# Where the triangular solve of the gated DeltaNet branch is started among the forgetting-attention tiles of a hybrid encoder step

## The chip, the cores and the metric

The kernel runs on 1 core of a Trainium2 chip. The metric is the time of one execution on the device in microseconds (us). Five engines run their own instruction queues: TensorE (PE, with its weight loads shown as PEld), VectorE (DVE), ScalarE (ACT), GpSimd (POOL) and SyncE (SP, which issues most DMAs). Each works its queue in the order in which the program was built; semaphores hold an instruction until what it needs is there.

## The reference, cut to what matters

One layer for two request groups (a prompt of 1024 rows and a sample of 64 rows behind a cache of 256). Four branches read one projection of the normed input; then come their gates, the merge, the output projection and a SwiGLU block.

```python
def fox_core(q_args, q_pos, k, v, ck, k_pos):            # forgetting attention ("fox")
    s = einsum('bqhd,bkhd->bhqk', q, k) * HEAD_DIM ** -0.5
    s = s + cq[..., :, None] - ck[..., None, :]
    p = softmax(where(k_pos <= q_pos, s, -inf))
    return einsum('bhqk,bkhd->bqhd', p, v)
...
a = p[:, :, 0] - lam * p[:, :, 1]                        # differential attention ("diff")
...
m = where(strict, einsum('nbhid,nbhjd->nbhij', kb, kc) * decay, 0.0)   # gated DeltaNet ("gdn")
sol = triangular_solve(m + eye(chunk), rhs, lower=True, unit_diagonal=True)
S, o = lax.scan(step, s0, (qc, kc, u0, kcum, gcum, qk))  # sequence over the 64-row chunks
...
merged = sum(gate[:, :, i] * (o @ wb[i]) for i, o in enumerate(branches))
```

## The kernel before, in words

Rows are worked in tiles of 128 (t = 0 to 7 of the prompt, t = 8 the sample). Attention runs branch by branch: sb (stick-breaking), then fox, then diff; within a branch by pair of heads (0, 1), within a pair over the tiles in the order 7, 6, 5, 4, 3, 2, 8, 1, 0. A tile t of the prompt has W = 128 (t + 1) keys, the sample 320. Below, "fox 0.4" is tile 4 of pair 0 of the fox branch.

A fox tile, for each of its two heads: PE writes scores into a PSUM bank `psc` (L456, L460; three such banks), DVE takes them out with one custom operation that adds the bias and keeps the running minimum ("score sum", L570), ACT takes the exponential, ACT and DVE write the two halves of the probability `st`, SP turns it with a transposing DMA into `pt`, and PE multiplies it with the values (`pv`, L468). A diff head takes four or two score banks, a maximum on DVE (L646, into `sm`), an exponential on ACT (L655, into `p`), some small DVE operations, `st`, the transposing DMA, and PE's `po` (L604, L606).

Between the attention instructions PE gets dense work that waits for nothing there: `spill_gates` computes the gates of all four branches in 96 pieces of 24 matmuls (`pgs`, L183 to L185), which ACT evicts as `ths` and POOL's queue writes to DRAM as `gtd`. A third stream is the list `side`: three generators, of which each call of `fill` advances the first by one step. `gdn_solve` loads the blocks `X` from DRAM (L871), does 30 steps of two DVE operations each (`tmpx` and `X`, L67) and stores the result (`xd`, `xtd`); `gdn_seq` then runs the sequence over 17 chunks on PE, DVE and ACT (`vn`, `vh`, `S32p`, `Sl`, `ztg`, `osg` are its DVE results); `open_merge` opens the pool of the merge and loads the sb branch's part of it. `fill` is called once in each fox tile and once in each diff head, before the multiplication with the values.

The merge comes last: 96 pieces of 6 matmuls (`ptb`), a tanh on ACT of the gate read back from DRAM (`thg`), and products and sums into `mg` on DVE and POOL. Its sb part (24 pieces) may start once `open_merge` has run; the fox, diff and gdn parts need the memory that attention gives back at its end.

The order on each engine isn't written out by hand: the code is traced, and a scheduler puts the traced instructions of each engine in an order by its own timeline, the earlier traced first among those it takes for ready. `issue_after(x)` forbids a block's instructions to stand ahead of `x` on the engine of `x`. So a step that is traced earlier shifts everything behind it.

Of the kernel before, what the change touches and what calls it, by code (L numbers as in the profile page):

```python
# [13 lines left out]
ALU = mybir.AluOpType  # L14
# [34 lines left out]
def rows(t):  # L49
    return P if t < 8 else SMP  # L50
# [3 lines left out]
def tile_hybrid_encoder(ctx, tc, i, o):  # L54

    nc = tc.nc
    act, vec, gps, pe, sync = nc.scalar, nc.vector, nc.gpsimd, nc.tensor, nc.sync


    def acopy(out, in_, scale=1.0):  # L60
        return act.activation(out, in_, AF.Copy, scale=scale)  # L61

    def stt(out, in0, s, in1, op0, op1):
        return vec.scalar_tensor_tensor(out=out, in0=in0, scalar=s, in1=in1, op0=op0, op1=op1)  # L64

    def tt(out, in0, in1, op, eng=None):
        return (eng or vec).tensor_tensor(out=out, in0=in0, in1=in1, op=op)  # L67

    def ts(out, in0, s1, s2, op0, op1=None, eng=None):
        if op1 is None:  # L70
            return (eng or vec).tensor_scalar(out=out, in0=in0, scalar1=s1, scalar2=None, op0=op0)  # L71
        return (eng or vec).tensor_scalar(out=out, in0=in0, scalar1=s1, scalar2=s2, op0=op0, op1=op1)

    def bc(ap, shape):
        return ap.to_broadcast(shape)
# [13 lines left out]
    def psc(name="psc"):  # L89
        return pp.tile([P, 512], F32, tag="s", name=name, bufs=3)  # L90
# [178 lines left out]
    for t in range(NT):  # L269
        n = rows(t)  # L270
# [45 lines left out]
    for t0, cols in (((0, 1, 2, 3), 0), ((4, 5, 6, 7), 512), ((9, 10, 8), 1024)):  # L316
        ps = psc("pct")
        c = 0
        for t in t0:
            n = SMP if t == 8 else P  # L320
# [107 lines left out]
    def qgeom(t):  # L428

        if t < 8:  # L430
            return P, 0, (t + 1) * P, [(j, P) for j in range(t + 1)]
        return SMP, SEQ, PAST + SMP, [(8, P), (9, P), (10, SMP)]

    def chunks(W):
        return [(c, min(512, W - c)) for c in range(0, W, 512)]

    def p_tiles(W, n):

        nb = (W + P - 1) // P
        st = at.tile([P, 2, 1024], F16, tag="st", name="st", bufs=3)  # L440
        sv = st.rearrange("p a b -> p (a b)")[:, :2 * nb * P].rearrange("p (a b) -> p a b", a=2)
        if W % P:
            vec.memset(sv[:n, :, W:], 0.0)
        pt = at.tile([P, 16, P], F16, tag="pt", name="pt", bufs=4)

        def transpose():
            sync.dma_start_transpose(out=pt[:, 0:2 * nb, 0:n], in_=sv[:n].rearrange("p a b -> p (a b)"))
            return lambda hl, j, ks: pt[:ks, hl * nb + j, 0:n]

        return sv, transpose  # L450

    def scores(ps, n, w, q0, q1, kk, col, mask, diag):

        two = q1 is not None
        last = mask is None and not two
        pe.matmul(ps[:n, :w], lhsT=q0, rhs=kk[:, col:col + w], start=True, stop=last)  # L456
        if mask is not None:
            pe.matmul(ps[:n, diag:diag + n], lhsT=identb[:n, :n], rhs=mask[:n, :n], start=False, stop=not two)
        if two:
            pe.matmul(ps[:n, :w], lhsT=q1, rhs=kk[:, col:col + w], start=False, stop=True)  # L460
# [14 lines left out]
    def load_kv(b, pair):  # L475
        nk = 4 if b == "diff" else 2
        kT = []
        for q in range(0, nk, 2):
            k2 = at.tile([P, 2, KW], F16, tag="k", name="kT", bufs=3)
            sync.dma_start_transpose(out=k2, in_=kd_[b][:, (pair * nk + q) * P:(pair * nk + q + 2) * P])  # L480
            kT += [k2[:, 0], k2[:, 1]]
        vt = at.tile([P, 11, 2, 2, 64], F16, tag="v", name="vt", bufs=2)
        v3_ = vt.rearrange("p t h l e -> p t (h l e)")
        cs = slice(pair * 256, (pair + 1) * 256)
        sync.dma_start(v3_[:, 0:10], vd[b][0:SEQ + PAST, cs].rearrange("(t p) c -> p t c", p=P))
        sync.dma_start(v3_[:SMP, 10], vd[b][SEQ + PAST:, cs])
        return kT, vt

    def load_q(b, pair, t, n):
        qt = at.tile([P, 4, P], F16, tag="qt", name="qt", bufs=3)  # L490
        sync.dma_start_transpose(out=qt[:, :, 0:n], in_=qd[b][t * P:t * P + n, pair * 512:(pair + 1) * 512])
        return qt


    dense, side = [], []
# [21 lines left out]
    at_mark = [None]  # L517
# [34 lines left out]
    def attend_fox():  # L552
        for pair in range(2):
            kT, vt = load_kv("fox", pair)
            ckb = cb.tile([P, 2, KW], F32, tag="ckb", name="ckb", bufs=1)
            for hp in range(2):
                gps.dma_start(ckb[:, hp], ckd[2 * pair + hp].partition_broadcast(P))
            for t in QORD:
                n, kc, W, vl = qgeom(t)
                qt = load_q("fox", pair, t, n)  # L560
                pts = []
                for hp in range(2):
                    s = at.tile([P, 1024], F32, tag="wk", name="s", bufs=6)
                    mn = at.tile([P, 4], F32, tag="sm", name="mn", bufs=6)
                    for c, (c0, w) in enumerate(chunks(W)):
                        ps = psc()
                        diag = W - n - c0 if c0 + w == W else None
                        scores(ps, n, w, qt[:, 2 * hp, :n], qt[:, 2 * hp + 1, :n], kT[hp], kc + c0,
                               mk_fox if diag is not None else None, diag)
                        vec.tensor_tensor_reduce(  # L570
                            out=s[:n, c0:c0 + w], in0=ps[:n, :w], in1=ckb[:n, hp, kc + c0:kc + c0 + w], scale=0.125,
                            scalar=(3e38 if c == 0 else mn[:n, c - 1:c]), op0=ALU.add, op1=ALU.min,
                            accum_out=mn[:n, c:c + 1])
                    act.activation(s[:n, :W], s[:n, :W], AF.Exp, scale=-1.0, bias=mn[:n, c:c + 1], accum_out=mn[:n, 2:3])
                    vec.reciprocal(mn[:n, 3:4], mn[:n, 2:3])
                    ts(mn[:n, 3:4], mn[:n, 3:4], PS, None, ALU.mult)
                    sv, tr = p_tiles(W, n)
                    acopy(sv[:n, 0, :W], s[:n, :W], mn[:n, 3:4])
                    at_mark[0] = stt(sv[:n, 1, :W], s[:n, :W], mn[:n, 3:4], sv[:n, 0, :W], ALU.mult, ALU.subtract)
                    pts.append(tr())  # L580
                fill(FILL_FOX * W)
                pv_pair("fox", pair, t, n, vt, vl, pts)
# [281 lines left out]
    def gdn_solve():  # L864


        NP = 17 * NH
        with tc.tile_pool(name="gp2", bufs=1, side="right", reuse_waits="tile") as g2p:
            X = g2p.tile([NP, 2, 32, 32], F32, name="X")
            tmp = g2p.tile([NP, 512], F32, name="tmpx")  # L870
            gps.dma_start(X.rearrange("p b j i -> p b (j i)"), nd[0:17, :, 0:2].rearrange("n h b j i -> (n h) b (j i)"))  # L871
            for _ in range(2):
                yield 0.0
            for j in range(1, 31):
                r = 31 - j
                behind = tc.issue_after(at_mark[0].ins) if j == 1 else ExitStack()
                behind.__enter__()
                tj = tmp[:, :2 * j * r].rearrange("p (b c i) -> p b c i", b=2, c=j)
                tt(tj, bc(X[:, :, 0:j, j:j + 1], [NP, 2, j, r]), bc(X[:, :, j:j + 1, j + 1:32], [NP, 2, j, r]), ALU.mult)
                tt(X[:, :, 0:j, j + 1:32], X[:, :, 0:j, j + 1:32], tj, ALU.add)  # L880
                behind.__exit__(None, None, None)
                if j % 4 == 0:
                    yield 0.0
            for q in range(2):
                vec.memset(X[:, q].rearrange("p j i -> p (j i)")[:, 0:1024:33], 1.0)
            gps.dma_start(xd, X.rearrange("p b j i -> p (b j i)"))
            for q in range(2):
                vec.tensor_copy(tmp.rearrange("p (i j) -> p i j", j=32),
                                X[:, 0, :, 16 * q:16 * q + 16].rearrange("p j i -> p i j"))
                gps.dma_start(xtd[:, 512 * q:512 * q + 512], tmp)  # L890
# [231 lines left out]
    def open_merge():  # L1122
        gd_.close()
        brps.append(br_.enter_context(tc.tile_pool(name="br", bufs=1, side="right", reuse_waits="tile")))
        load_branch("sb")
        yield 0.0

    side += [gdn_solve(), gdn_seq(gd_), open_merge()]
    attend_fox()
    attend_diff()  # L1130
    drain(side)
# [154 lines left out]
    with tc.tile_pool(name="ps2", bufs=1, space=PSUM) as pf:  # L1286
# [189 lines left out]
        for t in (8, 0, 1, 2, 3, 4, 5, 6, 7):  # L1476
            n = rows(t)
# [54 lines left out]
```

## Time and profile before

| what | value |
|---|---|
| median of 3 runs | 1818.23 us (1810.99 to 1825.81) |
| profiled execution | 1816.62 us, span of its instructions 1814.9 us |
| granted TensorE clock, mean | 0.988 |
| PE busy | 1723.7 us (95%) |
| DVE busy | 1246.7 us (69%) |
| ACT busy | 866.9 us (48%) |
| POOL busy | 307.0 us (17%) |

The busy times are unions over the whole span. The stages differ: attention with the gates fills about 330 to 920 us, the merge about 920 to 1040 us, and after it come the output projection and the SwiGLU block, which the change doesn't touch.

### The profile page before, as it was taken

How to read it: one execution, taken by the hardware profiler on the slowest of the kernel's cores; microseconds unless marked ns; L12 is line 12 of the kernel's file. 1: busy time of each engine (PE TensorE's matmuls, PEld its weight loads, DVE VectorE, ACT ScalarE, POOL GpSimd, SP SyncE). 2: the span in 40 equal slices, each digit the busy share in tenths (PEclk: the TensorE clock that was granted, in tenths of full speed). 3: DMA queues.
4: the chain of work that ended last, by engine and by line, in shares of the span. 5: the costliest groups of instructions: out<-in, count | busy, mean ns of one | idle time of the engine just before them, and what ended most of it. 6: DMA issues, size and time to landing. Idle time of an engine off the chain costs nothing.

```text
span 1814.9 us, 36826 instructions
## 1 busy us (share of the span) xinstructions
PE 1723.7 (95%) x14364; PEld 1224.8 (67%) x14364; DVE 1246.7 (69%) x2589; ACT 866.9 (48%) x1819; POOL 307.0 (17%) x478
## 2 busy tenths in 40 slices
PE   7999898888998899999988899999999999999998
PEld 5678787765565566666655588768668578577573
DVE  7659875966678777877868877667555556365465
ACT  6336556986765465665665634424223124132132
POOL 2114241011121222322236611000000000000003
PEclk9999999998999999999999999999999999999999
DMA  7267689979699986765589555312112112112113
GB/s 231 50 100 200 205 239 243 212 181 180 142 226 199 184 199 149 160 154 147 122 280 290 165 154 109 88 49 64 52 47 71 47 47 70 35 36 70 35 48 105
DMA packets 412766, 244.28 MB, mean 135 GB/s; under 512 B 266278, under 2 KB 390450, under 8 KB 412456
## 3 DMA queue, kind: packets, MB, share of 16 engines
q1 hardware_dynamic: 398944, 205.67, 46.6%
q0 software_dynamic: 13648, 36.27, 7.1%
q8 instruction: 112, 1.84, 0.5%
q14 instruction: 62, 0.51, 0.1%
HBM read 123.39 MB, written 60.53 MB: 101 GB/s over the span
## 4 chain that ended last, share of the span: by engine, by line
PE 55%; DMA 6%; DVE 5%; issue 2%; ACT 1%; POOL 1%; SPq 0%; DVEq 0%; POOLq 0%; ACTq 0%
PE po L1454 12%; PE pgs L183 4%; PE pgs L185 4%; PE pgs L184 4%; PE pb L1337 3%; PE pb L1339 3%; PE pb L1338 3%; DMA pt<-st 3%; PE pa L1339 2%; PE pc L1338 2%; PE pa L1338 2%; PE pa L1337 2%; PE pc L1339 2%; PE pc L1337 2%; DMA thg<-gtd_sb 1%
## 5 line engine op out<-in xcount | busy, mean ns | idle before, releaser
L184 PE MATMUL pgs<-u,wh 128*128 128x364 f16 (+1 forms) x768 | 245.5, 320 | 0.0
L183 PE MATMUL pgs<-u,wh 128*128 128x364 f16 (+1 forms) x768 | 245.4, 319 | 0.0
L185 PE MATMUL pgs<-u,wl 128*128 128x364 f16 (+1 forms) x768 | 245.3, 319 | 0.0
L1454 PE MATMUL po<-wh,hT 128*128 128x512 f16 (+1 forms) x792 | 238.1, 380 | 0.6 <-DVE x2a L64 0.6
L1454 PEld LDWEIGHTS <-hT 128*128 128x128 f16 (+1 forms) x1188 | 109.2, 99 | 120.1 <-issue 7.6
L64 DVE SCALAR_TENSOR_TENSOR x2a<-po,x2a 128x512 f32<-128x512 f32 x108 | 74.4, 689 | 141.5 <-PE po L1454 141.3
L61 ACT ACTIVATE wh<-w32f 128x1024 f16<-128x1024 f32 (+1 forms) x90 | 80.3, 926 | 160.7 <-PE po L1454 111.7
L1337 PE MATMUL pb<-X,wh 128*128 128x288 f16 (+1 forms) x528 | 147.4, 280 | 2.5 <-DMA X<-nsh 2.2
L64 DVE SCALAR_TENSOR_TENSOR wl<-w32f,wh 128x1024 f16<-128x1024 f32 (+1 forms) x90 | 94.6, 1064 | 79.7 <-ACT wh L61 79.6
L1338 PE MATMUL pb<-X,wh 128*128 128x288 f16 (+1 forms) x528 | 147.7, 280 | 0.0
L1339 PE MATMUL pb<-X,wl 128*128 128x256 f16 (+1 forms) x528 | 146.8, 280 | 0.0
L1337 PEld LDWEIGHTS <-wh 128*128 128x128 f16 x1232 | 120.8, 98 | 31.6 <-issue 2.3
L1454 PE MATMUL po<-wl,hT 128*128 128x512 f16 (+1 forms) x396 | 142.0, 379 | 0.0
L1338 PEld LDWEIGHTS <-wh 128*128 128x128 f16 x1232 | 120.8, 98 | 30.3 <-issue 2.4
L1339 PEld LDWEIGHTS <-wl 128*128 128x128 f16 x1232 | 120.8, 98 | 27.0 <-issue 0.4
L165 PE MATMUL pd<-wh,u 128*128 128x256 f16 (+1 forms) x448 | 125.1, 279 | 4.4 <-DVE qs L64 2.3
L166 PE MATMUL pd<-wl,u 128*128 128x256 f16 (+1 forms) x448 | 125.0, 279 | 0.0
L167 PE MATMUL pd<-wh,u 128*128 128x256 f16 (+1 forms) x448 | 124.9, 279 | 0.0
L185 PEld LDWEIGHTS <-wl 128*128 128x128 f16 x912 | 89.7, 98 | 50.7 <-issue 2.7
L183 PEld LDWEIGHTS <-wh 128*128 128x128 f16 x912 | 89.8, 98 | 50.1 <-issue 0.7
L184 PEld LDWEIGHTS <-wh 128*128 128x128 f16 x912 | 89.8, 98 | 49.0 <-issue 0.9
L71 POOL TENSOR_SCALAR fss<-fss 128x1 f32<-128x1 f32 (+1 forms) x9 | 2.0, 220 | 661.8 <-ACT fsq L1483 661.8
(393 smaller groups left out, 4625.3 us busy)
## 6 DMA issues: line engine op xcount, KB each, us to landing
w<-in_w_in_dram SPq DMA_DIRECT2D x56, 512.0 KB, 5.0
w32f<-in_w_ffn_gate_dram SPq DMA_DIRECT2D x20, 512.0 KB, 5.0
w32f<-in_w_ffn_up_dram SPq DMA_DIRECT2D x20, 512.0 KB, 3.9
w32f<-in_w_ffn_down_dram SPq DMA_DIRECT2D x20, 512.0 KB, 4.3
xt<-in_x_prompt_dram SPq DMA_DIRECT2D x8, 512.0 KB, 6.7
wb<-in_w_branch_dram SPq DMA_DIRECT2D x8, 512.0 KB, 4.8
w<-in_w_out_dram SPq DMA_DIRECT2D x8, 512.0 KB, 5.4
x2a<-in_x_prompt_dram SPq DMA_DIRECT2D x8, 512.0 KB, 7.9
```

Of the source, the lines that this page charges most:

```text
L61: return act.activation(out, in_, AF.Copy, scale=scale)
L64: return vec.scalar_tensor_tensor(out=out, in0=in0, scalar=s, in1=in1, op0=op0, op1=op1)
L165: pe.matmul(ps[:n, :N], lhsT=a, rhs=wh[:, k, :N], start=(k == 0), stop=False)
L166: pe.matmul(ps[:n, :N], lhsT=a, rhs=wl[:, k, :N], start=False, stop=False)
L167: pe.matmul(ps[:n, :N], lhsT=b, rhs=wh[:, k, :N], start=False, stop=(k == K - 1))
L183: pe.matmul(ps[:, :n], lhsT=a, rhs=xh[:, k, off:off + n], start=(k == 0), stop=False)
L184: pe.matmul(ps[:, :n], lhsT=a, rhs=xl[:, k, off:off + n], start=False, stop=False)
L185: mm = pe.matmul(ps[:, :n], lhsT=b, rhs=xh[:, k, off:off + n], start=False, stop=(k == K - 1))
L1337: pe.matmul(ps[:, :n], lhsT=wh[:, k], rhs=xh_, start=(start and k == 0), stop=False, skip_group_check=not start)
L1338: pe.matmul(ps[:, :n], lhsT=wh[:, k], rhs=xl_, start=False, stop=False, skip_group_check=not start)
L1339: mm = pe.matmul(ps[:, :n], lhsT=wl[:, k], rhs=xh_, start=False, stop=(k == 3), skip_group_check=not start)
L1454: pe.matmul(ps[h * n:h * n + n], lhsT=hts[k + h][:, a, tk:tk + n], rhs=w[:, k + h], start=(k == 0 and a == 0 and w is wh), stop=(k + nh >= ...
```

## The change: what it does

It has three parts. `gdn_solve` yields once instead of twice behind its load of `X`. Its first step, which is that load, is taken with `next(side[0])` before fox is traced, so it stands ahead of fox's own loads. And the mark behind which the first solve step must stand (`at_mark`) is the last score sum of the tile instead of the last half of its probabilities. Together the solve's DVE steps are traced from the first fox tile on (before: from the third), and `gdn_seq` and `open_merge` move up by two calls of `fill` as well.

```diff
@@ attend_fox @@
-                        vec.tensor_tensor_reduce(
+                        at_mark[0] = vec.tensor_tensor_reduce(
                             out=s[:n, c0:c0 + w], in0=ps[:n, :w], in1=ckb[:n, hp, kc + c0:kc + c0 + w], scale=0.125,
...
-                    at_mark[0] = stt(sv[:n, 1, :W], s[:n, :W], mn[:n, 3:4], sv[:n, 0, :W], ALU.mult, ALU.subtract)
+                    stt(sv[:n, 1, :W], s[:n, :W], mn[:n, 3:4], sv[:n, 0, :W], ALU.mult, ALU.subtract)
@@ gdn_solve @@
-            for _ in range(2):
-                yield 0.0
+            yield 0.0
@@ tile_hybrid_encoder @@
     side += [gdn_solve(), gdn_seq(gd_), open_merge()]
+    next(side[0])
     attend_fox()
```

No instruction is added or removed; the order changes. Lines behind the first edit in `gdn_solve` are one lower in the changed kernel (L1067 becomes L1066) as far as `attend_fox()`.

DVE, the first tile of fox (7 of pair 0), from its last score sum (L570, the second row of which only reads its minimum out) on. Before:

```order
L570 ISA s,mn<-psc,ckb,mn 128x512
L570 ISA mn 128x1
L575 RECIPROCAL mn<-mn 128x1
L64 SCALAR_TENSOR_TENSOR os<-pv,os 128x128
L71 TENSOR_SCALAR mn<-mn 128x1
L570 ISA s,mn<-psc,ckb 128x512
```

Now:

```order
L570 ISA s,mn<-psc,ckb,mn 128x512
L570 ISA mn 128x1
L67 TENSOR_TENSOR tmpx<-X 68x60
L575 RECIPROCAL mn<-mn 128x1
L64 SCALAR_TENSOR_TENSOR os<-pv,os 128x128
L67 TENSOR_TENSOR X<-X,tmpx 68x2x30
L71 TENSOR_SCALAR mn<-mn 128x1
L67 TENSOR_TENSOR tmpx<-X 68x116
```

The solve starts right behind the first tile's score sums. Before the last `st` of fox 0.4 stood 10 of its 60 operations, now 30; before the last `st` of fox 0.1 stood 22, now 50.

PE, from the last gate matmul (`pgs`) on, at the end of attention (LDWEIGHTS are weight loads). Before:

```order
L185 MATMUL pgs<-u_103,wl 128x360
L183 LDWEIGHTS wbh
L183 MATMUL ptb<-oT,wbh 128x364
L184 LDWEIGHTS wbh
L184 MATMUL ptb<-oT,wbh 128x364
```

Now:

```order
L606 MATMUL po<-vt,pt 128x64
L456 LDWEIGHTS qt
L456 MATMUL psc<-kT,qt 128x384
L458 LDWEIGHTS identb
L458 MATMUL psc<-mk_diff,identb 128x128
```

Before, the sb part of the merge follows the last gate and only the last three `po` groups of diff (of pair 1: second head of tile 1, both heads of tile 0) stand among it. Now the piece shown stands 36 rows behind the last gate: behind that gate come 8 `ptb`, the last `po` of diff 1.4, and then the 16 scores of diff 1.2, 1.8, 1.1 and 1.0 with all their `po` and those of diff 1.3 (62 `po` matmuls in all, 8 before). Ahead of the last `po` stand 11 `ptb` pieces now, 9 before, and 14 `ptb` matmuls have moved ahead of the last gate.

ACT, the eviction of the last gate piece (`ths`) and what is next to it; `sm_12700` holds the sums of the first head of diff 1.2, `sm_12763` of its second, `sm_12620` of diff 1.3's second. Before:

```order
L1167 ACTIVATE thg<-thg 128x364 x2
L61 ACTIVATE wh<-w_14096 128x1024
L61 ACTIVATE osd<-o_12838 64x128
L61 ACTIVATE ths<-pgs 128x360
L1167 ACTIVATE thg<-thg 128x360
```

Now:

```order
L61 ACTIVATE ths<-pgs 128x360
L61 ACTIVATE st<-p,sm_12620 128x512
L61 ACTIVATE t_12537<-po 128x64
L655 ACTIVATE p,sm_12700<-psc,sm_12700 128x384
L614 ACTIVATE sq<-o_12341 128x128
L655 ACTIVATE p,sm_12700<-psc,sm_12700 128x384
L655 ACTIVATE p,sm_12763<-psc,sm_12763 128x384
```

Before, no exponential of attention is left behind the last gate; now 16 are.

## Rows read from the trace of the kernel before

**Rows 1.** The page, busy time by engine (share of the span, instructions)

```profile
PE 1723.7 (95%) x14364; PEld 1224.8 (67%) x14364; DVE 1246.7 (69%) x2589; ACT 866.9 (48%) x1819; POOL 307.0 (17%) x478
```

**Rows 2.** Windows: length, busy us of each engine, granted clock, DMA share, GB/s

```profile
420.00:440.00 20.00, 13.33 (x110) 8.22 (x111) 9.17 (x10) 9.59 (x17) 1.77 (x3) 0.74 0.96 177
500.00:620.00 120.00, 107.79 (x1024) 67.76 (x1024) 94.94 (x304) 66.58 (x149) 23.99 (x40) 0.99 1.04 208
640.00:920.00 280.00, 277.32 (x2827) 187.52 (x2828) 224.47 (x712) 166.01 (x445) 82.60 (x138) 1.00 0.66 157
880.00:920.00 40.00, 40.00 (x361) 26.34 (x360) 32.87 (x127) 24.87 (x75) 14.54 (x25) 1.00 0.56 140
920.00:1040.00 120.00, 102.79 (x669) 63.17 (x668) 94.86 (x161) 71.93 (x142) 64.00 (x65) 0.99 0.84 254
```

**Rows 3.** What PE waited for, 495 to 940 us: total, times, longest

```profile
PE psc L456 <- DVE mn L570: 6.7, 3, 3.7
PE po L604 <- DMA pt<-st: 2.7, 2, 1.5
PE pv L468 <- DMA pt<-st: 2.3, 3, 1.2
```

**Rows 4.** Tile X: count, duration ns min/median/max, first and last start

```profile
L67 DVE TENSOR_TENSOR tmpx<-X x30: 209/524/648, 518.4 to 599.7; 68x60 f32<-68x60 f32 x2, 68x116 f32<-68x116 f32 x2, 68x168 f32<-68x168 f32 x2, 68x216 f32<-68x216 f32 x2
L67 DVE TENSOR_TENSOR X<-X,tmpx x30: 217/526/646, 518.6 to 600.0; 68x60 f32<-68x60 f32 x2, 68x116 f32<-68x116 f32 x2, 68x168 f32<-68x168 f32 x2, 68x216 f32<-68x216 f32 x2
L871 POOL DMA_DIRECT2D X<-nd x1: 571/571/571, 406.2 to 406.2; - x1
...
DMA to landing us min/median/max: 5.5/10.3/15.2
```

**Rows 5.** Timeline: fox 0.7's last score sum; fox 0.4's last st; its first pv

```profile
495.68 0.74 DVE L570 CUSTOM_DVE_ANT_0 s<-psc,ckb,mn 128x512 f32<-128x512 f32 x1
...
524.62 0.88 DVE L64 SCALAR_TENSOR_TENSOR st<-s,mn,st 128x640 f16<-128x640 f32 x1
...
529.98 0.24 PE L468 MATMUL pv<-pt,vt 128*64 128x128 f16 x1
```

**Rows 6.** Timeline of PE: the last gate matmul, the next two, the last po

```profile
925.68 0.32 PE L185 MATMUL pgs<-u,wl 128*128 128x360 f16 x1
925.83 0.32 PE L183 MATMUL ptb<-oT,wbh 128*128 128x364 f16 x1
925.99 0.32 PE L184 MATMUL ptb<-oT,wbh 128*128 128x364 f16 x1
...
936.81 0.19 PE L606 MATMUL po<-vt,pt 128*128 128x64 f16 x1
```

**Rows 7.** Timeline of DVE: first maximum of diff 1.2, last st of diff 1.0

```profile
883.15 0.55 DVE L646 TENSOR_REDUCE sm<-psc 128x1 f32<-128x384 f32 x1
...
917.67 0.35 DVE L64 SCALAR_TENSOR_TENSOR st<-p,sm,st 128x128 f16<-128x128 f32 x1 [0.52 <-ACT st L61]
```

**Rows 8.** DVE groups between these two: busy us, mean ns, idle before

```profile
L64 DVE SCALAR_TENSOR_TENSOR wl<-w,wh 128x1024 f16<-128x1024 f32 x2 | 2.5, 1225 | 0.4 <-ACT wh L61 0.4
...
L64 DVE SCALAR_TENSOR_TENSOR st<-p,sm,st 128x512 f16<-128x512 f32 x2 | 1.5, 740 | 0.0
...
L64 DVE SCALAR_TENSOR_TENSOR S32p<-pog,S 128x256 f32<-128x256 f32 x2 | 0.8, 418 | 0.0
...
L67 DVE TENSOR_TENSOR osg<-ztg,osg 128x256 f16<-128x256 f32 x1 | 0.4, 425 | 0.1
```

**Rows 9.** The chain that ended last, around diff 1.5's second st: start, us

```profile
847.72 0.20 DVE Sl L64
847.92 6.59 DMA pt<-st
854.55 0.23 PE po L604
```

**Rows 10.** Tile mg: the sb part's products on DVE (24 pieces)

```profile
L64 DVE SCALAR_TENSOR_TENSOR mg<-thg,ptb x24: 518/529/534, 929.5 to 963.5; 128x364 f32<-128x364 f32 x16, 128x360 f32<-128x360 f32 x8
```

## The prediction

> **What bounds the kernel now.** I read the busy times first: PE is busy 1723.7 us, 95% of the span, DVE 69% [rows 1]. An average hides the stages, so next the windows. From 640 to 920 us PE is busy 277.3 of 280 us at granted clock 1.00 [rows 2]: the reader is to see that whatever DVE, ACT or the DMA queues do there costs nothing while PE has something dense to do, and that PE's work is the same after the change, since no instruction is added or removed. Only two stretches that the change touches have idle time of PE: 500 to 620 (fox), 120 − 107.8 = 12.2 us, and 920 to 1040 (end of diff and merge), 120 − 102.8 = 17.2 us [rows 2]. The third view is what PE waited for in attention: three waits of score banks for DVE's score sums, 6.7 us, three short waits of fox's `pv` for the turned probabilities, 2.3 us, and two of diff's `po`, 2.7 us [rows 3]. So there is little that an earlier solve could give back, and the question is what its new order uncovers.
>
> **What moves.** The solve's 60 DVE operations ran from 518.4 to 600.0 us, about 0.525 us each, spread by the calls of `fill`. Their blocks had long landed: the load was issued at 406.2 and takes at most 15.2 us [rows 4]. So the earlier request is worth nothing (the wait for it is nil), and of the three edits it is the mark and the dropped step that act: the first step may now start at 495.68 + 0.74 = 496.4 us, behind the last score sum of fox 0.7 [rows 5], 22 us earlier. The sequence over the chunks and the opening of the merge follow from it. The DMAs that they issue move along on SP's and POOL's queues (the solve's store, the sequence's loads, the sb loads): the sequence alone waits for the store, and has moved with it; nothing waits for the sb loads before the merge.
>
> What is traced earlier stands earlier on every engine, and the order shows what is pushed back: on PE the diff tiles stand behind some 33 to 46 us more work, against the gates, which are the dense filler. The gates therefore run out while diff isn't done. Before, behind the last gate stood 8 `po` matmuls and no exponential; now 62 `po` matmuls, 16 scores and 16 exponentials. That is where the main cost is.
>
> **The terms**, against the profiled execution (1816.62 us).
>
> (1) The tail of diff. Before, from the end of the last gate (925.8) to the last `po` (936.8) were 11.0 us [rows 6], filled with sb pieces of the merge. Now PE first has 8 `ptb` matmuls, 10 `po` and the first score of diff 1.2, about 8 × 0.155 + 0.4 + 0.4 = 2 us (0.155 is the distance of two starts in [rows 6]). Then it follows DVE through diff 1.2, 1.8, 1.1 and 1.0. How long DVE takes for these I take from their run before: first maximum at 883.15, last `st` at 918.02, 34.9 us [rows 7]. In it stood work that has now moved ahead: some twelve operations of the sequence at about 0.42 each (5.0 us), one `wl` of 1.2 and one `st` of 0.7 [rows 8]; two products of the merge of 0.53 are added [rows 10]. 34.9 − 5.0 − 1.2 − 0.7 + 1.1 = 29 us. From the last `st` to its `po` the transposing DMA takes what it took at diff 1.5, 847.72 to 854.55, 6.8 us [rows 9]. So 2 + 29 + 6.8 = 38 us in place of 11.0: **+27**. Low end: DVE was busy 32.87 of 40 us there [rows 2], so without idle time 29 × 0.82 = 24, +22. High end: the whole 34.9, +33. PE's own sb pieces can't cover it: only 11 of them stand ahead of the last `po` (9 before).
>
> (2) The last gate ends earlier, since the scores and `po` now behind it (about 4.7 us of PE, 16 scores and 54 `po` at their durations) left, and 14 `ptb` came ahead (14 × 0.155 = 2.2): **−2.5**.
>
> (3) The two waits of diff's `po`, 2.7 us [rows 3], stood where a tile now has 33 us more of filler ahead of it: **−2.7**, bound 0.
>
> (4) The merge behind the last `po` has two sb pieces fewer. The 15 pieces from 936.8 to 963.5 [rows 6, 10] took 26.7 us, 1.8 each: **−3.6**. Bounds: 0, and −14.6 if the other 13 (23.1 us) went at PE's own pace, 13 × 6 matmuls of 0.155 = 12.1 us (a gain of 11.0 more).
>
> (5) Fox. DVE now has 30 solve operations ahead of fox 0.4's last `st` (10 before) and 50 ahead of fox 0.1's (22 before): 20 × 0.525 = 10.5 us of work earlier. Its cover is DVE's idle time, 120 − 94.9 = 25 us in the stretch [rows 2], and the distance from that `st` (524.62) to its `pv` on PE (529.98) [rows 5], to which some 7.6 us of PE work are added, two gate pieces of 3.7 us (24 × 0.155) among it. If the cover is gone, the score banks are late: a wait as those in [rows 3], up to 3.7 us, twice: +8. If the later tiles gain what the solve no longer takes from them, the 12.2 us of idle go but for 2: −10. Both signs are open, and I take **0**.
>
> (6) The clock. From 420 to 440 us PE was busy 13.3 of 20 us, and the granted clock was 0.74 [rows 2]; in the tail only some 13 of 38 us are left for it to do. But DVE paces the tail, and a slower matmul shows only in the links between the engines: **0**, bound +5 (13 / 0.74 − 13 = 4.6). [...]
>
> Sum: 27 − 2.5 − 2.7 − 3.6 + 0 + 0 = +18.2, 1816.6 + 18.2 = 1834.8 us. The profiled execution is 1.6 us below the median of the three runs, so **1836 us**, +1.0% on the median.
>
> **The rivals.** *Idle time goes (not slower).* DVE's serial work is done earlier, so fox's later tiles and the merge no longer wait, and the idle 12.2 + 17.2 = 29.4 us of [rows 2] falls to about 2. Against a tail at its low end: 22 − 2.5 − 2.7 − 27 = −10, 1808 us; with the tail at 27, 1813. It decides from a fall of the idle time by some 20 us. For it: most of the wait time in fox is for DVE [rows 3]. Against: the merge's idle time is at pieces that need gates read back from DRAM and memory that attention gives back, and neither comes earlier. Price taken: 1811.
>
> *The change doesn't matter.* PE is full, its work is the same, and what looks like an uncovered tail is covered by the 11 sb pieces and the 17.2 us idle that are there already: 1818. For it: 277.3 of 280. Against: the order's 62 `po` behind the last gate, which wait for DVE whatever PE does.
>
> *DVE falls behind in fox.* 50 of the solve's operations lie ahead of pair 1's score sums, PE waits there for three more banks of about 3.5 us each, as long as the longest so far [rows 3], +10: 1846. For it: DVE is 79% busy in that stretch already. Against: its 25 us of idle time.
>
> *The clock falls in the tail and stays low into the merge*: +5, 1841.
>
> **How the numbers follow.** Forecast .50, no effect .15, idle goes .15, DVE behind .15, clock .05. A measurement of this kernel can tell about 1% from no change: faster is below 1800, slower above 1836.4. The forecast lies on the upper bound: half of it (.25) is slower, half the same. Idle goes: .05 faster, .10 same. No effect: .15 same. DVE behind and clock: .20 slower. So faster .05, same .50, slower .45. Range: from 1812 (the lower half of the rival with the idle time, .07, is out) to 1853 (the tail's +33 with fox's +8 and half of the clock's bound, less 8.8, comes to 1853; what lies above has about .08).
>
> **What would show it.** Windows of the changed kernel: behind the last `pgs` a stretch of 35 to 40 us with PE about a third busy, DVE at 80% or more, waits of `po` for `pt` and of `psc` for DVE's maxima in the list of waits, and a granted clock below 1. The last gate should end near 923, the last `po` near 961, the solve's `X` should start near 496. Term 5 is read from 500 to 620: idle PE 12 us as before, or 2, or 20. I am wrong if the last `po` follows the last gate by under 25 us, if PE is as idle as before from 920 to 1040, or if the last gate itself ends more than 5 us from 923, which would be fox's doing.

## The result, and the profile after

The changed kernel took 1840.28 us (median of 4 runs, 1837.93 to 1850.25), the kernel before 1814.61 us beside it: a ratio of 1.0153 over the runs (95% interval 1.012 to 1.0185), slower by 1.5%; the two medians alone differ by 25.7 us. The forecast was 1836 us, +1.0% on the median shown, with a range of 1812 to 1853. The profiled execution after is 1837.93 us, its span 1836.2 us, 21.3 longer than that of before. Each of the two kernels was profiled a second time among the experiments (`before_again`, `after_again`); what follows rests on both pairs where a difference is under 10 us.

The page after, busy time by engine, answers to [rows 1]:

```profile
PE 1729.8 (94%) x14364; PEld 1228.6 (67%) x14364; DVE 1251.1 (68%) x2589; ACT 866.2 (47%) x1819; POOL 304.4 (17%) x478
```

Windows after, for [rows 2], with the tail of diff by itself (923 to 958); the columns are those of [rows 2]:

```profile
420.00:440.00 20.00, 20.00 (x201) 12.97 (x202) 15.37 (x17) 18.48 (x31) 3.54 (x6) 1.00 0.94 201
500.00:620.00 120.00, 104.90 (x1039) 66.42 (x1036) 85.05 (x259) 58.05 (x127) 24.47 (x41) 0.99 0.93 187
640.00:920.00 280.00, 274.35 (x2665) 183.65 (x2663) 209.80 (x618) 157.37 (x405) 75.47 (x126) 1.00 0.66 165
923.00:958.00 35.00, 22.25 (x144) 13.13 (x143) 28.02 (x122) 21.14 (x69) 7.72 (x14) 0.66 0.56 123
920.00:1040.00 120.00, 94.19 (x584) 56.63 (x582) 94.11 (x236) 70.04 (x168) 51.34 (x58) 0.87 0.78 212
```

In the tail PE is busy 22 of 35 us, and that at a mean granted clock of 0.66; DVE is busy 80% there. This is the stretch that the order had shown without gates.

PE's timeline after, the last gate matmul and the last `po`, for [rows 6]:

```profile
922.92 0.32 PE L185 MATMUL pgs<-u,wl 128*128 128x360 f16 x1
...
957.97 0.19 PE L606 MATMUL po<-vt,pt 128*128 128x64 f16 x1
```

From the end of the one (923.24) to the end of the other (958.16) are 35 us. In the second profile they are 941.3 to 976.3, 35.0 again; in both profiles of before 11.0. DVE's timeline after, first maximum of diff 1.2 (three in a row) and last `st` of diff 1.0, for [rows 7]:

```profile
925.99 1.48 DVE L646 TENSOR_REDUCE sm<-psc 128x1 f32<-128x384 f32 x3
...
950.86 0.34 DVE L64 SCALAR_TENSOR_TENSOR st<-p,sm,st 128x128 f16<-128x128 f32 x1
```

The chain that ended last shows what PE follows in there. From one score to the next it runs through DVE's maxima, an exponential on ACT and back (start, us, what):

```profile
935.81 0.42 PE psc L456
936.25 0.49 DVE sm L646
...
936.99 0.24 DVE p L64
937.23 0.21 issue
937.59 0.32 DVE sm L646
...
938.70 0.28 DVE sm L646
938.98 0.52 DVE st L64
...
942.38 0.65 ACT p L655 x3
...
944.29 0.26 PE psc L456
```

Of the chain's 34.9 us in the tail, DVE's pieces are 11.8, three DMAs 10.4 (two transposing ones of 5.59 and 2.45, a gate read back of 2.40) and PE's 7.8. So the tail isn't DVE's work alone.

What PE waited for after, 495 to 940 us, for [rows 3] (total, times, longest):

```profile
PE pv L468 <- DMA pt<-st: 11.1, 8, 2.5
PE psc L456 <- ACT p L655: 5.4, 5, 3.7
PE po L604 <- DMA pt<-st: 4.4, 4, 2.7
PE py L962 <- DMA t<-xtd: 3.6, 1, 3.6
PE psc L456 <- DVE mn L570: 3.6, 2, 2.3
```

Fox's `pv` now waits 11.1 us for the turned probabilities, 2.3 before; by the order, the solve's operations now stand ahead of the `st` that feed them. The sequence's first `py` waits 3.6 us for what the solve has just stored. The waits for score sums went from 6.7 to 3.6 here; in `before_again` they were 10.7 (440 to 640 us) and in `after_again` 5.2, so a single profile says little of their size.

The two stages, in two profiles of either kernel (windows, columns as above).

Before:

```profile
440.00:900.00 460.00, 443.27 (x4369) 290.47 (x4367) 357.50 (x1067) 274.54 (x675) 111.84 (x188) 1.00 0.77 169
900.00:1100.00 200.00, 182.79 (x1418) 130.26 (x1416) 156.46 (x291) 105.35 (x211) 83.47 (x95) 0.99 0.73 212
```

Before, profiled again:

```profile
440.00:900.00 460.00, 441.14 (x4327) 288.64 (x4325) 353.72 (x1050) 273.64 (x669) 110.91 (x185) 0.99 0.77 167
900.00:1100.00 200.00, 182.52 (x1402) 127.98 (x1401) 155.12 (x303) 104.64 (x215) 85.67 (x96) 0.98 0.73 210
```

After:

```profile
440.00:900.00 460.00, 436.01 (x4256) 285.82 (x4254) 336.96 (x975) 259.06 (x627) 110.89 (x185) 1.00 0.76 173
900.00:1100.00 200.00, 168.71 (x1232) 114.02 (x1230) 157.93 (x353) 103.08 (x235) 77.63 (x89) 0.92 0.64 179
```

After, profiled again:

```profile
440.00:900.00 460.00, 434.88 (x4234) 283.97 (x4233) 335.06 (x950) 259.25 (x618) 109.53 (x183) 0.98 0.78 171
900.00:1100.00 200.00, 169.01 (x1215) 110.39 (x1213) 153.46 (x367) 106.41 (x254) 77.51 (x90) 0.93 0.68 192
```

The length less PE's busy time is its idle time. From 440 to 900 us it was 16.7 and 18.9 before, 24.0 and 25.1 after: 6.8 more. From 900 to 1100 it was 17.2 and 17.5, then 31.3 and 31.0: 13.8 more, and there the clock fell besides, 0.99 and 0.98 to 0.92 and 0.93. So the loss has two places, and the larger one is the tail.

The smaller one isn't all fox. Fox's last `pv` ended at 647.5 and 655.1 us before, at 661.0 and 677.9 after. From 440 us to that `pv` PE was idle 14.1 and 17.5 us, then 20.5 and 20.5: 4.7 more. The other 2.0 us lie behind it, in diff.

### The profile page after: what moved, and what is told of

Read it like the earlier page. It is cut to its first block, busy times and chain, and to the rows that moved or that the text cites. A ratio compares the mean times of both kernels' runs of the same rounds, so it can differ in the third digit from the quotient of the medians.

```text
span 1836.2 us, 36833 instructions
## 1 busy us (share of the span) xinstructions
PE 1729.8 (94%) x14364; PEld 1228.6 (67%) x14364; DVE 1251.1 (68%) x2589; ACT 866.2 (47%) x1819; POOL 304.4 (17%) x478
```

## The experiments

Two theories stood against each other. **T**: the time is lost at the end of diff, because the gates run out on PE while DVE still paces the last tiles. **F**: it is lost from fox on, because the solve's DVE work comes early. (The first two expectations also name M, the mark itself.) The table has every profile: the ratio to the kernel before on the same chip, the start of the solve's first operation, PE's idle time from 440 to 900 us, how much of it lies up to fox's last `pv`, the time from the end of the last gate matmul to the end of the last `po`, and PE's idle time from 900 to 1100 us (all in us).

| kernel | ratio (interval) | solve from | idle 440–900 | of it in fox | gate to po | idle 900–1100 |
|---|---|---|---|---|---|---|
| before, twice | | 518.4, 520.0 | 16.7, 18.9 | 14.1, 17.5 | 11.0, 11.0 | 17.2, 17.5 |
| changed, twice | 1.0153 (1.012–1.0185) | 486.1, 499.0 | 24.0, 25.1 | 20.5, 20.5 | 35.0, 35.0 | 31.3, 31.0 |
| mark_only | 1.0090 (1.0057–1.0123) | 506.6 | 21.6 | 15.9 | 10.3 | 20.3 |
| steps_old_mark | 1.0176 (1.0142–1.0211) | 496.8 | 25.3 | 12.7 | 8.7 | 33.3 |
| sequence_held | 1.0197 (1.0166–1.0228) | 495.0 | 23.6 | 21.2 | 23.3 | 26.3 |
| last_four_held | 1.0244 (1.0199–1.0288) | 495.4 | 23.6 | 18.9 | 6.9 | 30.5 |
| before_gates_early | 1.0186 (1.0133–1.0239) | 510.4 | 19.4 | 16.8 | 42.7 | 40.6 |
| gates_spread | 1.0176 (1.0129–1.0223) | 492.7 | 30.4 | 26.5 | 13.2 | 32.4 |
| seq_where_it_was | 1.0118 (1.0083–1.0154) | 499.0 | 26.8 | 24.1 | 12.3 | 23.0 |
| seq_later_still | 1.0172 (1.0149–1.0195) | 496.2 | 33.8 | 26.1 | 3.8 | 29.4 |
| before_seq_later | 1.0044 (1.002–1.0068) | 519.9 | 21.0 | 16.6 | 2.7 | 15.8 |
| merge_loads_held | 1.0147 (1.0121–1.0172) | 504.9 | 26.2 | 18.0 | 14.5 | 23.7 |

The idle columns leave the clock out. From 440 to 900 us its mean was 1.00 and 0.99 before, 1.00 and 0.98 in the changed kernel, 0.97 in `steps_old_mark`, `seq_later_still` and `merge_loads_held`, and 0.98 or 0.99 in the others. By an estimate, 0.02 of 460 us are some 9 us, so differences of that size in time can stand there without any idle time.

**mark_only**: the first of the three edits alone (both lines of `at_mark`).

> Only the mark is moved to the last score sum; the two steps and the place of the load are as before. 15 of the solve's operations stand ahead of fox 0.4's last st (before 10, changed kernel 30); behind the last gate stand 8 po matmuls and no score (before 8 and none, changed kernel 62 and 16). Theory T (the time is lost at the end of diff, where the gates have run out): no uncovered tail, so within 6 us of before, last gate to last po about 11 us. Rival F (the time is lost because the solve's DVE work comes early in fox): a quarter of the operations have moved, so a quarter of the loss, +5 to +7 us, and last gate to last po still 11 us. Rival M (it is the mark itself, each of whose waits now ends earlier or later on DVE): the whole +20 to +27.

1831.32 us against 1817.26, 14.1 more. The tail is as before (10.3 us), and yet 0.9% is lost: T alone doesn't hold. F had said 5 to 7 us and M 20 to 27, so no theory has the number. Idle time from 440 to 900 us is 21.6, between the two kernels, but up to fox's last `pv` it is 15.9, as before; the rest is in diff, where `po` waited 5.6 us for `pt` (2.7 and 1.4 before). The profiled execution was the fastest of the four (1825.94 us).

**steps_old_mark**: the other two edits alone.

```diff
-            for _ in range(2):
-                yield 0.0
+            yield 0.0
...
+    next(side[0])
     attend_fox()
```

> The load is taken ahead of fox and one step is dropped, but the mark stays at the last half of the probabilities. 24 of the solve's operations stand ahead of fox 0.4's last st (before 10, changed kernel 30), so most of its move is there; but no score and only 8 po stand behind the last gate. This tells the theories apart best. T: within 6 us of before, last gate to last po 9 to 14 us. F: 14 of 20 operations moved, +14 to +19 us, as idle time of PE from 500 to 640 us. M: no loss at all, and none either if only the mark of the changed kernel is put back.

1845.98 us, 28.7 more than before and as slow as the changed kernel or slower, with no tail behind the last gate and with the old mark. T's number failed outright, and M is out. F failed in the place that it had named: from 500 to 640 us PE was idle 12.0 us, 12.2 and 16.1 before, and up to fox's last `pv` 12.7. Of the 25.3 us of idle time, 12.6 stand in diff (2.7 and 1.4 before). There is a third cost that no theory had, waits of diff's `po` for `pt`. The list of waits of this kernel, 640 to 880 us and 880 to 960 us:

```profile
PE po L604 <- DMA pt<-st: 10.8, 4, 5.5
...
PE po L604 <- DMA pt<-st: 13.5, 1, 13.5
```

Its chain there (start, us, what):

```profile
891.79 0.79 DVE st L64
892.61 18.95 DMA pt<-st
911.60 0.29 PE po L604
```

One transposing DMA took 18.95 us from issue to landing, where the median is 3.7 (860 to 960 us). The two loads of `w_branch` and the two gate read-backs that stand next to it on SP's queue were issued behind it, and from 900 to 920 us the DMA engines' share was 1.01. SP's issues:

```profile
892.61 3.11 SPq L447 DMA_TRANSPOSE pt<-st  x1
896.37 1.04 SPq L1116 DMA_DIRECT2D wb<-in_w_branch_dram  x2
```

The window of that wait:

```profile
900.00:920.00 20.00, 8.40 (x49) 5.08 (x49) 6.08 (x13) 7.19 (x13) 0.56 (x1) 0.66 1.01 224
```

The opening of the merge had moved up among diff's last transposes. It also loads `oT` on POOL's queue: four loads of 544 KB, issued from 892.3 to 894.5 us, of which the last landed at 911.1, just ahead of the end of that wait. In both profiles of either kernel, too, the longest transposing DMA from 850 to 960 us was under way beside these four loads (9.4, 9.4, 7.5 and 8.8 us; medians 3.1 to 3.8). `merge_loads_held` below follows that up.

**sequence_held**: the changed kernel with four empty steps at the head of `gdn_seq`.

```diff
     def gdn_seq(stack):
+        for _ in range(4):
+            yield 0.0
```

> The changed kernel, with four empty steps ahead of the sequence over the chunks: the solve is where the changed kernel has it (30 operations ahead of fox 0.4's last st), but 7 scores and 36 po stand behind the last gate instead of 16 and 62. T: about half the tail, last gate to last po some 20 to 25 us instead of 35, and a time 8 to 14 us over before. F: no change against the changed kernel, +20 to +27 over before, since the solve hasn't moved back.

The tail was 23.3 us, as T had it from the order (7 scores for 16), but the time was 1852.08 us, 34.8 over before: no better than the changed kernel, where T had said 8 to 14 over before and F no change. The shorter tail didn't show in the time; the last gate itself ended at 943.5 us, 14 us later than the mean of before. From 440 us to that gate PE was idle 26.3 us, 16.7 and 18.9 before, at a mean clock of 0.98 for 1.00 and 0.99: some 8 us of idle time, and by an estimate (0.015 of 503 us) up to 7 us of clock.

**last_four_held**: gate pieces 93 to 96 held behind the score written last where they are drawn (the scores of diff set `sc_mark`, `npg` counts the pieces).

```diff
-                gemm_a(pg, wu, m * P, uh, ul, off, n, KD)
+                with (tc.issue_after(sc_mark[0].ins) if npg[0] > 92 else ExitStack()):
+                    gemm_a(pg, wu, m * P, uh, ul, off, n, KD)
```

> The changed kernel, but the matmuls of the last four gate pieces (93 to 96) may not stand ahead of the score that was written last where they are drawn. Up to them the order on PE is that of the changed kernel; then the four pieces (4 x 3.7 = 15 us of PE work) stand between the last po groups, and only 4 po are left behind the last gate. T: PE was idle 12.8 of 35 us in the tail and its clock was halved there; with the four pieces in it the last po comes 12 to 15 us sooner against the rest, so 11 to 16 us faster than the changed kernel and 6 to 12 slower than before, and the granted clock of the tail is back above 0.9. F: no change against the changed kernel, since fox is the same to the last instruction.

1857.75 us, 2.4% over before, where T had said 11 to 16 us faster than the changed kernel. The pieces were drawn after the last score of diff, so they stood behind all 16 scores and between the `po`, where nothing waited for DVE:

```profile
921.00:949.00 28.00, 14.05 (x85) 7.80 (x84) 23.86 (x107) 17.72 (x58) 2.04 (x5) 0.57 0.40 81
949.00:974.00 25.00, 24.81 (x169) 15.27 (x167) 12.93 (x50) 9.69 (x29) 9.19 (x16) 0.94 0.36 98
```

The scores ran uncovered from 921 to 949 us (14 us idle, clock 0.57), and the four pieces came after them as work in series. The column "gate to po" is short here for that reason alone: it measures the tail only where nothing else is put in it.

**before_again, after_again**: the two kernels unchanged.

> The kernel before, profiled once more. In its first profile PE lost 8 us more in the stick-breaking stage (up to 440 us) than the changed kernel, and 9 us less from 440 to 900 us. mark_only, whose order up to fox is that of before row by row, lost 5 us less there, so much of the first difference should be chance. If the 9 us of fox and diff are the solve's, they stand here again (lost time from 440 to 900 us within 3 us of the first profile); if they are chance too, they move by 5 us or more.

> The changed kernel, profiled once more, for the spread of a stage between two executions. If its losses are made by its order, the time lost by PE from 440 to 900 us and from 900 to 1080 us is within 4 us of its first profile (60 and 50 us), and the stage up to 440 us, which has little of the change, may move by as much as 8.

The "lost time" of these two expectations is no view shown here; what follows is PE's idle time. From 440 to 900 us it moved by 2.2 and 1.1 us between two profiles, the tail by nothing, while the stage ahead of fox (300 to 440 us) had 23.0 and 20.2 us before, 15.7 and 24.8 after. So the difference of the stage up to 440 us is chance, and favoured the first profile of the changed kernel by 7 us; the other two differences came out again, and are put down to the order.

**before_gates_early**: the kernel before with one number changed.

```diff
-FILL_SB, FILL_FOX, FILL_DIFF, FILL_GDN = 0.0143, 0.006, 0.0155, 8
+FILL_SB, FILL_FOX, FILL_DIFF, FILL_GDN = 0.0143, 0.006, 0.0280, 8
```

> The kernel before, with the solve and fox where they are, but gates drawn faster in diff (0.0280 for 0.0155): 20 scores and 62 po stand behind the last gate, as in the changed kernel (16 and 62). Theory T (the tail of diff without gates costs some 20 us whoever uncovers it): last gate to last po 32 to 40 us, and +14 to +24 us over before. Rival F (the loss is made by the early solve in fox): no change from before, within 5 us.

1851.52 us against 1818.93, +1.9%, though solve, sequence and fox stand as before and idle time from 440 to 900 is that of before (19.4). The time grew by 32.6 us and the tail by 31.7, to 42.7 us:

```profile
928.00:971.00 43.00, 24.94 (x161) 14.62 (x160) 34.66 (x142) 26.14 (x83) 8.94 (x16) 0.72 0.53 126
```

This shows T's mechanism by itself, without the solve, and at more than its expected size.

**gates_spread**: the changed kernel, the last seven pieces held each behind a score of its own; `HOLD` is a table from piece to score.

```diff
+    HOLD = {90: (1, 2, 0, 0), 91: (1, 2, 0, 1), 92: (1, 2, 1, 1), 93: (1, 8, 0, 1), 94: (1, 8, 1, 1), 95: (1, 1, 0, 1), 96: (1, 1, 1, 1)}
...
-                gemm_a(pg, wu, m * P, uh, ul, off, n, KD)
+                with (tc.issue_after(sc_mark[HOLD[npg[0]]].ins) if npg[0] in HOLD else ExitStack()):
+                    gemm_a(pg, wu, m * P, uh, ul, off, n, KD)
```

> The changed kernel, but the last seven gate pieces are each held behind one score of diff 1.2, 1.8 or 1.1, so that they stand between these scores and not ahead of them (last_four_held had put them behind all scores). What is then without gates is shorter: 8 scores of diff 1.4 and 1.3. T: the 23 us in which PE follows DVE with nothing between become 8 to 12, so 8 to 14 us faster than the changed kernel, granted clock in 920 to 960 us above 0.9; what is left over before is fox's share. F: as slow as the changed kernel, within 4 us.

1850.55 us, where one run of the changed kernel beside it took 1855.18: no gain that can be told, where T had said 8 to 14 us. The tiles that got gates are covered, those that lost them are not (the first row below has diff 1.4 and 1.3):

```profile
907.00:935.00 28.00, 17.91 (x115) 10.04 (x114) 19.02 (x72) 14.93 (x42) 3.99 (x6) 0.76 0.37 84
...
935.00:962.00 27.00, 27.00 (x209) 17.43 (x208) 22.03 (x91) 17.15 (x55) 7.95 (x13) 1.00 0.61 138
```

The hole moved forward and kept 10 us of idle time at a clock of 0.76. The filler is finite; what is put into the tail is missing ahead of it.

**seq_where_it_was**: the changed kernel with twelve empty steps at the head of `gdn_seq`, so that the sequence stands where before had it, and the solve where the change put it.

> The changed kernel with twelve empty steps ahead of the sequence over the chunks (four, in sequence_held, had moved it too little). The solve is where the changed kernel has it (30 operations ahead of fox 0.4's last st), the sequence's matmuls stand between 549 and 759 us of PE work (before 547 to 760, changed kernel 520 to 714), and behind the last gate stand no score and 12 po. This parts the two costs. T (the tail comes from the sequence's place, not from the solve's): last gate to last po 10 to 16 us and PE idle from 900 to 1080 us 17 to 21 us as before (changed kernel 31). F, as it stands after two profiles of either kernel (7 us more idle time of PE from 440 to 900 us): if the early solve makes it, it stays, +5 to +12 us on before; if the early sequence makes it, it goes, within 4 us of before.

1838.78 us against 1817.06. The tail is back at 12.3 us, so it belonged to the place of the sequence and not to that of the solve; idle time from 440 to 900 stayed at 26.8 (24.1 of it up to fox's last `pv`), so that share isn't the sequence's. PE's waits there, 440 to 640 us:

```profile
PE pv L468 <- DMA pt<-st: 9.1, 8, 3.8
PE psc L456 <- DVE mn L570: 8.5, 4, 3.9
```

`pv` waits 9.1 us for `pt`, as in the changed kernel (9.6 and 8.2), against 4.1 and 2.7 before and 1.8 in `before_gates_early`. But the time gained little on the changed kernel (1.0118 for 1.0153, the intervals overlap), and the loss of 21.7 us is larger than F's range of 5 to 12. From 440 us to the first `pa` of the feed-forward block PE was idle 50.4 us, where the changed kernel has 55.9 and 56.8 and the kernel before 34.5 and 36.9: 11.6 us less in the tail than in the changed kernel, but 3.6 more ahead of the last gate and 2.0 more in the merge. Most of the merge's share against before is one wait right behind the last `po` (900 to 1130 us; its longest is 1.9 in both profiles of before):

```profile
PE ptb L183 <- DVE mg L64: 9.4, 6, 6.1
```

On DVE that product into `mg` stands behind the closing operations of diff's last tile, which themselves waited 0.98, 0.96 and 1.88 us for POOL and ACT.

**seq_later_still**: fourteen empty steps.

> As seq_where_it_was with fourteen empty steps: the sequence stands between 563 and 782 us of PE work, later than before, 4 po behind the last gate, and no piece of the merge ahead of the last po (before 9, changed kernel 11). T: no tail at all, the last po within 6 us of the last gate; but all 24 sb pieces now lie behind attention, whose idle time in the merge (17 us before) may grow. Sum within 8 us of before, either way. F with the solve as its cause: +5 to +12.

1848.07 us, 31.0 over before: both forecasts failed, T's "within 8 us" and F's 5 to 12. The tail is gone (3.8 us), the merge pays for it: the first matmul of its sb part waited 9.2 us for `oT`, and from the last `po` to the first `pa` of the feed-forward block were 212.6 us, 190.8 and 192.0 before. That is some 21 us more behind the last `po` for 7 us less ahead of it, so the sb pieces ahead of the last `po` are worth some 14 us net. The rest is ahead of the last gate: idle time from 440 to 900 us was 33.8.

**before_seq_later**: the kernel before with six empty steps there.

> The kernel before with six empty steps ahead of the sequence, the solve untouched: 2 po behind the last gate (before 8), 5 sb pieces ahead of the last po (before 9), the sequence ends at 751 us of PE work (before 760). By T there is nothing to win beyond the 11 us from last gate to last po, which were busy with sb pieces: within 5 us of before. If it is clearly faster, the sequence's place was not at its best before either.

1825.41 us, +0.4% and 8.4 us, clear of no change (interval 1.002 to 1.0068) and over the 5 us that had been allowed: nothing to win, and a little to lose.

**merge_loads_held**: `steps_old_mark`, with the opening of the merge behind diff's last transposing DMA on SP's queue.

```diff
-            sync.dma_start_transpose(out=pt[:, 0:2 * nb, 0:n], in_=sv[:n].rearrange("p a b -> p (a b)"))
+            tr_last[0] = sync.dma_start_transpose(out=pt[:, 0:2 * nb, 0:n], in_=sv[:n].rearrange("p a b -> p (a b)"))
...
-    side += [gdn_solve(), gdn_seq(gd_), open_merge()]
+    side += [gdn_solve(), gdn_seq(gd_), ]
...
     drain(side)
+    with tc.issue_after(tr_last[0].ins): side += [open_merge()]; drain(side)
```

> steps_old_mark, whose tail was covered by its order and which yet lost 13.5 us in one wait of po for pt, with the opening of the merge held behind the last transposing DMA of diff on SP's queue. On PE the end of attention is then that of before (8 po behind the last gate, 9 sb pieces ahead of the last po). If that wait was a transposing DMA queued behind the merge's loads (w_branch, w_out, gates read back), it goes: no wait of po over 4 us, and 12 to 20 us faster than steps_old_mark, +5 to +14 on before. If it was chance, the time stays at +25 to +30.

The wait of 13.5 us is gone (no wait of `po` for `pt` over 3.1 us), as it should be if the merge's loads made it. But the time fell from 1.0176 to 1.0147 only, some 5 us where 12 to 20 had been said, and +25.5 us on before is where the expectation had put chance. The tail grew from 8.7 to 14.5 us, and 8.2 us of waits of `po` for `pt` remain from 640 to 900 us. So the loads are the likely cause of that wait, by this run and by the transposing DMAs beside them in the other profiles; that they cost the time isn't shown.

## Why the prediction was right

By its own steps; means of two profiles where both kernels have two.

**(1) The tail**, +27 forecast, +24.0 measured (35.0 for 11.0). Of its parts, PE's rest ahead of DVE took 2.8 us for 2, and DVE's stretch 25.2 (925.99 to 951.20, DVE busy 22.5 of it) for 29. The estimate from DVE's earlier run was 4 us too long, within the bounds given. The way from the last `st` to its `po` took 7.0 for 6.8, but that is luck: the transposing DMA that was to fill it took 2.3 us from issue to landing. Sb pieces on PE and two waits for DVE's `o` filled the rest (SP's issue and PE's last wait):

```profile
951.75 1.17 SPq L447 DMA_TRANSPOSE pt<-st  x1
...
957.92 0.22 PE L604 MATMUL po<-vt,pt 128*128 128x128 f16 x1 [0.63 <-DVE o L64]
```

What no run shows is that taking the tail away gives its 24 us back: the kernels without one (`steps_old_mark`, `seq_where_it_was`, `seq_later_still`) are 21 to 31 us slower than before, for losses of their own ahead of it and behind it. That a tail costs its length by itself is shown by `before_gates_early`.

**(2), (3), (5)** together set when the last gate ends: −5.2 forecast, +3.1 measured (923.2 and 941.3, before 926.0 and 932.3). The step that failed is (5), fox, which I had taken at 0 and bounded by −10 and +8: idle time up to fox's last `pv` grew by 4.7 us. The cover that I named, DVE's idle time and the PE work between `st` and `pv`, didn't suffice. In the stretch that I had named for reading it, 500 to 620 us, it hardly shows (12.2 and 14.8 us idle before, 15.1 and 15.8 after); fox now ends 14 and 23 us later. That it goes with the solve's place is shown in part. Up to fox's last `pv` the four profiles with the solve from 510 us on have 14.1 to 17.5 us, the seven profiles with all three edits 18.9 to 26.5, and bringing the sequence back alone didn't change it. But `mark_only` has 15.9, and the two kernels with an early solve and the old mark have 12.7 and 18.0: it takes the edits together, and why stays open. (3) was wrong as well: diff's waits for `pt` from 640 to 900 us went from 2.7 and 1.4 to 1.8 and 2.2, and its idle time up to 900 us grew by 2.0. What is left for (2) after these 6.8 us and the chance of the stage ahead of fox (−1.4) is −2.3, but the clock ahead of the gate isn't in that sum, so no run shows (2).

**(4) The merge**, −3.6 forecast, +0.6 measured: from the last `po` to the first `pa` 190.8 and 192.0 us before, 192.4 and 191.5 after. Two pieces more ahead of the last `po` gave nothing; PE still waited 12.0 and 10.6 us there for the products of read-back gates (11.8 and 11.2 before), and its longest wait for `mg`, right behind the last `po`, grew from 1.9 to 4.1 us in both pairs. So a price per piece was the wrong model.

**(6) The clock** fell in the tail to a mean of 0.66, and to 0.50 from 930 to 950 us, with PE busy 5.45 us in the first half of this stretch and 6.92 in the second. PE's 22.3 busy us are more than the 13 that I had counted, and still less than DVE's 28.0. But 6.3 us of PE's pieces on the chain stand where the clock was 0.50. From one start of a `ptb` matmul to the next were 0.30 us there (950 to 951 us) and 0.155 at 1.00 (953 to 956); by an estimate from these two the 6.3 us would have been half at 1.00, so the clock cost up to some 3 us of the tail. That is within the bound of 5; the 0 itself isn't shown.

The sum measured is 24.0 + 3.1 + 0.6 = 27.7 us, and the ratio of the runs, 1.0153, is 27.8 us on the profiled execution's 1816.6. The forecast was 18.2: the tail was sized well, the terms ahead of the last gate and the merge were taken some 8 and 4 us too low. The two errors don't change the sign, and the range held them. That the forecast of 1836 us lies only 4 us below the 1840.28 is partly luck: beside the changed kernel the kernel before took 1814.61 us, 3.6 less than the median that the forecast was added to. The first pair of profiles alone, +21.3, would have flattered the forecast, by 7 us of chance ahead of fox.

Of the signs named ahead, the stretch behind the last gate (35.0 us for 35 to 40), DVE's share (80%) and the clock below 1 came true. PE was busy 64% there and not a third, at a mean clock of 0.66, and `psc` waited for ACT's exponentials (6.5 us) rather than for DVE's maxima (0.8). The last gate ended at 923.2 us in the first profile, but at 941.3 in the second, more than 5 us from 923, which the prediction had called fox's doing; 9 of these 18 us are idle time from 300 to 440 us, which is chance.

Of the rivals, "the change doesn't matter" and "idle time goes" are out; "DVE falls behind in fox" is partly true beside the tail, though by late `pt` and not by score banks. "The clock stays low into the merge" is out too: from the last `po` to the first `pa` its mean was 0.98 in both profiles, 0.99 and 0.98 before. What stays open: why diff's `po` wait longer for `pt` in `mark_only`, `steps_old_mark` and `merge_loads_held`, and which of the three edits costs how much, since each part by itself lost more than the theories gave it.

## What to carry to other kernels

Where one engine is full because a finite amount of dense filler lies between the steps of a latency-bound chain, ask first what stands behind the last piece of filler: a chain that ends later than the filler shows in the time (the stretch grew by 24.0 us here, and in `before_gates_early` by 31.7 us with 32.6 us of time), and holding some pieces back only moved the hole. Moving the work back doesn't return the time by itself: what is uncovered elsewhere has to be read again. Work brought forward on a second engine because its data is there wasn't free here, where that engine feeds the first one: DVE had been 79% busy from 500 to 620 us, and PE's idle time in fox grew by 4.7 us. And a load stream that moved up with it came among the transposes that the chain waits for: one of them took 18.95 us in `steps_old_mark`, where the median is 3.7.

## What was not expected of the hardware

- One transposing DMA of `steps_old_mark` took 18.95 us instead of a median of 3.7. Beside it four loads of 544 KB were under way on POOL's queue and two of 512 KB on SP's, and the DMA engines were at a share of 1.01 (224 GB/s) from 900 to 920 us; in that one wait PE was idle 13.5 us, and the granted clock was 0.66 from 900 to 920 us. In the four profiles of the two kernels the transposing DMA beside the same four loads took 7.5 to 9.4 us.
- A stage whose order is the same row by row on PE and DVE (`mark_only` and before, up to fox) had 23.0, 20.2 and 17.1 us of idle time of PE from 300 to 440 us in three executions, mostly in seven or eight waits of `pv` for such a DMA (18.6, 14.5 and 13.0 us in all, 8.3 the longest). Differences of 5 us between two profiles mean nothing there.
